# A planner that books small tiles and parameter tables in pieces of 2 or 4 columns instead of 128

## The chip, the cores and the metric

One core of one Trainium2 chip. The time is device microseconds (us) of one execution of the program. The engines: PE (TensorE, matmuls and transposes), DVE (VectorE), ACT (ScalarE), POOL (GpSimd), and SP (SyncE), whose queue issues the loads of the weights.

## The reference

A two-layer backbone in fp32 over 256 latent tokens of width 2048 and 256 context tokens. Layer 0 is neighbourhood attention beside a bidirectional state-space scan, with one common input projection; layer 1 is a gated short convolution. Both start with an adaptive norm.

```python
def adaln(cond, w, b):
    m = jax.nn.silu(cond) @ w + b
    return jnp.split(m, 3, axis=-1)

def reference(x, c, ctx, c_ctx, ada_w, ada_b, norm_g, ...):
    for i in range(DEPTH):                                  # DEPTH = 2
        ...
        shift, scale, gate = adaln(c, ada_w[i], ada_b[i])
        h = modulate(rms_norm(x, norm_g[i]), shift[:, None], scale[:, None])      # h*(1+scale)+shift
        if needs_ctx:                                       # layer 0
            shift_c, scale_c, gate_c = adaln(c_ctx, ada_w[i], ada_b[i])
            hc = modulate(rms_norm(ctx, norm_g[i]), shift_c, scale_c)
        if i % 2 == 0:
            y, yc = na_ssd_mixer(h, hc, na_ssd_w_in[e], ...)        # p = h @ w_in; pc = hc @ w_in[:, K..]
            # attention over a window and the context; softplus(dt + bias); scans both ways; @ w_out
        else:
            y = short_conv_mixer(h, sc_w_in[o], sc_conv_w[o], sc_w_out[o])
        x = x + gate[:, None] * y
    return x
```

## The kernel before

**Numbers.** Every fp32 weight block is split into a rounded high part `wH` (a cast on ACT, line L458) and a low part `wL` = weight - `wH` (a subtraction on DVE, L465). The activations have `hH` and `hL` likewise. A product is three matmuls into one PSUM bank: high by high, low by high, high by low. All matmuls are issued by the helper `mm` (L231), all transposes on PE by `turn` (L235), so that these two lines stand for nearly all of PE's work. In the rows of the trace the moving operand is named first, so `bank<-wH,hH` is a projection with the weights moving (K, V, Q) and `bank<-hH,wH` one with the tokens moving (B).

**Buffers.** Weights are loaded in blocks of 128 x 1024 (512 KB) into `raw` buffers (five, and at the start four more that lie in tiles used later: two `PT`, `xtm`, `yi`). Three pairs `wH`/`wL` hold the blocks in use. There are eight PSUM banks. `issue()` (L428) puts the next load into SP's queue as soon as the planner has given back a raw buffer.

**The order.** Nothing reorders the program after it is written: each engine's queue runs in the order in which the code emits instructions, and semaphores only make an engine wait. The emission order comes from a planner. The work is a fixed chain of matmul loops plus many small generators (tasks) in three queues (`urgent`, `side`, `back`); a task yields what it needs next, for instance `("DVE", tile)`, and `pump()` lets it go on once `may()` finds that the engine's booked time and the time at which the tile is ready lie near PE's booked time. `force()` runs the task that is ready first until a condition holds. Each emitted instruction is booked by `plan.add` (called `E`) with a cost; the class `Plan` keeps, per piece of a tile, the time at which it is written (`w`) and until when it is read (`r`). What a piece is, `Plan.keys` says: it turns the columns that an instruction touches into numbers of pieces of 128 columns. The planner's times decide the order and nothing else; the waits that keep the results right come from the tile framework.

**Tables.** `small` (436 columns, conditioning vectors, norm gains, biases) and `const` (866 columns: the identity, `mhalf` = 32 columns of -0.5 at columns 130 to 161, masks) come in two loads each: the first 96 columns of `small` and the first 162 of `const` at the very start, the rest (L565, L566) behind the tokens of the context. `rstd` (L604) computes 1/sqrt through `mhalf` on POOL.

**The first stage** (to about 110 us). `x_load`, `x_norm` and `x_pair` load four row tiles of tokens (t = 0, 1 latent, 2, 3 context), sum squares (L636 on ACT, L638 on DVE), scale them (`xs`, L648 and L650), transpose them (`turn`) and copy the result to `xm` (L663 ACT, L664 DVE). `ada_gen` goes through the modulation in blocks j = 0..7 of 256 columns, in two parts A (scale) and S (shift): 16 matmuls of 256 columns with `cpad` as weights, of which the trace shows each as two rows (in the order four raw buffers of a part, a row each), a copy to `half` (L768 ACT), two transposes of `half`, a reduction on DVE (L776) and adds (L779 to L782) into the 32-column tiles `A0` and `S0`; then for the two rows of block j `hH` = S + A x on ACT (L798), the same unrounded to `tmp` on DVE (L800), and `hL` = `tmp` - `hH` (L804). The main loop goes through the same j: K and V for four row tiles, Q for two, B; the partial results of K and V are added up in SBUF by `part_gen` (L828 copy for j = 0, L830 add on DVE from j = 1; K lies in `sz` and `gt`, V in `Vt`). `spawn(back, gemv_gen())` computes the later modulation rows on DVE (L857) with loads of its own.

**dt_gen** (about 230 to 260 us) turns the dt projection into softplus(dt + bias): it loads the 128-column table `rows` (L1184) into a `half` buffer, adds the projection's halves (L1201) and the table (L1203) and goes on with Abs, Exp and a series on DVE (L1209 to L1222; L1210 is a reciprocal).

Of the kernel before, what the change touches and what calls it, by code (L numbers as in the profile page):

```python
# [37 lines left out]
class Plan:  # L38
# [11 lines left out]
    def keys(self, ap):  # L50
        a, n = ap.ap, ap.tensor.name
        if type(ap.tensor).__name__ == "Tile" and not n.startswith("dram"):
            lo = ap.offset % a[0][0] if a[0][0] else ap.offset
            hi = lo + sum(abs(s) * (c - 1) for s, c in a[1:])
            return [(n, u) for u in range(lo // 128, hi // 128 + 1)]
        if n.startswith("in_") or n.startswith("out_"):
            return []
        hi = ap.offset + sum(abs(s) * (c - 1) for s, c in a)
        return [(n, u) for u in range(ap.offset // 256, hi // 256 + 1)]
# [1944 lines left out]
```

## Time and profile before

| what | value |
|---|---|
| three timed runs | 1763.7, 1769.15, 1769.4 us, median 1769.15 |
| the profiled execution | 1762.67 us |
| its span (first to last instruction) | 1760.9 us |
| busy share of the span: PE, DVE, ACT, POOL | 98%, 73%, 45%, 11% |
| moved by DMA | 412.5 MB, mean 234 GB/s |
| granted clock of TensorE, mean | 0.999 |

A profile row of a timeline has the start, the duration, the engine (SPq is SP's DMA queue, PEld the weight load of a matmul), the line, the operation, the outputs and inputs with shapes and types, the count, and in brackets the idle time ahead of it with what ended it. A row of the windows has the window, its length, the busy time and count of PE, PEld, DVE, ACT and POOL, the granted clock, the DMA share and GB/s. A row of the waits has the total, how many, and the longest. Matmuls overlap: one with 512 columns takes 0.39 to 0.5 in a row, but starts 0.23 after the one before it.

### The profile page before, as it was taken

The numbers are of one execution on the slowest core, as the hardware profiler recorded it, in microseconds if no ns is written. First come the engines' busy times: TensorE is split into PE (matmuls) and PEld (weight loads), VectorE is DVE, ScalarE is ACT, GpSimd is POOL, SyncE is SP. The second block draws the span as 40 slices with busy tenths as digits, with TensorE's granted clock in tenths as the row PEclk, the third lists the DMA queues.
The fourth block names the chain that finished last, engine by engine and source line by source line (L and its number), as shares of the span: only waits on it lengthen the run. The fifth ranks groups of instructions, "written<-read, shape, count | busy, mean of one in ns | idle before, by whom it ended". The sixth has DMA issues, their size and how long they took to land.

```text
span 1760.9 us, 25272 instructions
## 1 busy us (share of the span) xinstructions
PE 1728.3 (98%) x9305; PEld 1442.4 (82%) x9305; DVE 1292.8 (73%) x2041; ACT 785.3 (45%) x1186; POOL 191.0 (11%) x300
## 2 busy tenths in 40 slices
PE   6999999999999999999999999999999999999998
PEld 4677988889888889888888898888878888888887
DVE  5566877888787987786888698876667776766555
ACT  5422335454354453353453444654435444444442
POOL 0000111013111012111012101110000000000000
PEclk9999999999999999999999999999999999999999
DMA  9987675577876677866577767787766888876774
GB/s 349 344 291 252 214 227 181 181 214 241 261 227 201 190 219 248 262 193 204 170 239 227 215 188 226 224 261 253 268 216 232 265 281 266 267 248 216 219 231 158
DMA packets 147629, 412.50 MB, mean 234 GB/s; under 512 B 34304, under 2 KB 48272, under 8 KB 147504
## 3 DMA queue, kind: packets, MB, share of 16 engines
q1 hardware_dynamic: 132112, 366.64, 64.0%
q0 software_dynamic: 15392, 44.24, 8.0%
q8 instruction: 73, 1.20, 0.3%
q14 instruction: 52, 0.43, 0.1%
HBM read 386.53 MB, written 25.59 MB: 234 GB/s over the span
## 4 chain that ended last, share of the span: by engine, by line
PE 94%; DVE 2%; DMA 1%; ACT 1%; issue 1%; SPq 0%; POOL 0%; DVEq 0%; ACTq 0%; POOLq 0%
PE bank L231 93%; PE bank L235 1%; DVE wL L465 1%; DMA raw<-in_ada_w 0%; ACT wH L458 0%; DMA half<-in_rows 0%; DVE hL L804 0%; SPq L618 0%; DMA raw<-in_sc_in 0%; DVE tmp L1283 0%; DVE h L1729 0%; DVE tmp L800 0%; ACT h L1748 0%; ACT hH L798 0%; DVE xm L664 0%
## 5 line engine op out<-in xcount | busy, mean ns | idle before, releaser
L458 ACT CAST wH<-raw 128x1024 fp32r<-128x1024 f32 (+1 forms) x440 | 459.5, 1045 | 664.0 <-PE bank L231 559.6
L465 DVE TENSOR_TENSOR wL<-raw,wH 128x1024 fp32r<-128x1024 f32 (+1 forms) x440 | 532.2, 1213 | 257.4 <-ACT wH L458 255.0
L231 PE MATMUL bank<-hH,wH 128*128 128x256 f32 (+1 forms) x1040 | 341.0, 328 | 0.9 <-ACT wH L458 0.9
L231 PE MATMUL bank<-hL,wH 128*128 128x256 f32 (+1 forms) x1040 | 337.0, 324 | 0.0
L231 PE MATMUL bank<-hH,wL 128*128 128x256 f32 (+1 forms) x1024 | 331.4, 324 | 3.1 <-DVE wL L465 3.1
L231 PE MATMUL bank<-wH,h 128*128 128x512 f32 x1024 | 316.8, 390 | 1.7 <-DVE h L1729 1.7
L231 PE MATMUL bank<-wH,hH 128*128 128x512 f32 x640 | 256.0, 400 | 4.8 <-ACT hH L798 2.6
L231 PE MATMUL bank<-wL,hH 128*128 128x512 f32 x640 | 249.9, 391 | 0.3 <-DVE wL L465 0.3
L231 PE MATMUL bank<-wH,hL 128*128 128x512 f32 x640 | 249.3, 390 | 0.1
L231 PEld LDWEIGHTS bank<-wH,h 128*128 128x128 f32 x1024 | 191.9, 188 | 43.5 <-DVE h L1729 3.0
L231 PEld LDWEIGHTS bank<-hH,wH 128*128 128x128 f32 x1040 | 197.8, 190 | 18.9 <-issue 2.0
L231 PEld LDWEIGHTS bank<-hL,wH 128*128 128x128 f32 x1040 | 197.8, 190 | 15.8
L231 PEld LDWEIGHTS bank<-hH,wL 128*128 128x128 f32 x1024 | 194.6, 190 | 19.4 <-DVE wL L465 4.1
L857 DVE SCALAR_TENSOR_TENSOR acc<-raw,csil,acc 128x512 f32<-128x512 f32 x240 | 179.1, 746 | 30.9 <-DMA raw<-in_ada_w 27.2
L231 PE MATMUL bank<-wL,h 128*128 128x512 f32 x512 | 199.4, 389 | 0.2 <-DVE wL L465 0.2
L231 PE MATMUL bank<-wH,mix 128*128 128x512 f32 x512 | 160.9, 391 | 0.0
L231 PEld LDWEIGHTS bank<-wH,hH 128*128 128x128 f32 x640 | 120.1, 188 | 36.3 <-issue 7.2
L231 PEld LDWEIGHTS bank<-wH,hL 128*128 128x128 f32 x640 | 120.1, 188 | 25.4 <-DVE hL L804 0.6
L231 PEld LDWEIGHTS bank<-wL,hH 128*128 128x128 f32 x640 | 120.1, 188 | 25.0 <-DVE wL L465 1.1
L231 PEld LDWEIGHTS bank<-wL,h 128*128 128x128 f32 x512 | 96.1, 188 | 20.6 <-DVE wL L465 0.6
L231 PEld LDWEIGHTS bank<-wH,mix 128*128 128x128 f32 x512 | 96.1, 188 | 20.4 <-issue 0.5
L231 PE MATMUL bank<-wL,mix 128*128 128x512 f32 x256 | 99.7, 390 | 0.0
(276 smaller groups left out, 1856.5 us busy)
## 6 DMA issues: line engine op xcount, KB each, us to landing
raw<-in_w_in SPq DMA_DIRECT2D x209, 512.0 KB
raw<-in_ada_w SPq DMA_DIRECT2D x163, 512.0 KB
raw<-in_sc_in SPq DMA_DIRECT2D x128, 512.0 KB
raw<-in_w_out SPq DMA_DIRECT2D x64, 512.0 KB
raw<-in_sc_out SPq DMA_DIRECT2D x32, 512.0 KB
dram_ptd<-tmp POOLq DMA_DIRECT2D x32, 256.0 KB, 4.9
D<-dram_ptd POOLq DMA_DIRECT2D x64, 128.0 KB, 5.6
tmp<-dram_csr SPq DMA_DIRECT2D x32, 256.0 KB
```

Source lines behind the costliest of these rows:

```text
L231: E(T.matmul(o, l, r, start=start, stop=stop, skip_group_check=True))
L235: E(T.transpose(o, i, ident if k == 128 else ident[:k, :k]))
L458: E(S.copy(H, v))
L465: E(V.tensor_tensor(out=Lo, in0=v, in1=H.bitcast(F32), op=ALU.subtract))
L857: E(V.scalar_tensor_tensor(out=acc, in0=v[:, j], scalar=csil[:, 2 * k + j:2 * k + j + 1], in1=acc, op0=ALU.mult, op1=ALU.add))
```

## The change

`Plan.keys` cuts a tile into pieces of 4 columns if its rows are shorter than 256 elements (the sums of squares, `rx`, `A0`, `S0`, the statistics, the small rows of the gates), and of 2 columns if it is one of the two tables; all other tiles keep pieces of 128. The pieces of DRAM tiles, the kernel's arithmetic and the instructions are unchanged: each engine has the same ones as before.

```diff
         if type(ap.tensor).__name__ == "Tile" and not n.startswith("dram"):
             lo = ap.offset % a[0][0] if a[0][0] else ap.offset
             hi = lo + sum(abs(s) * (c - 1) for s, c in a[1:])
-            return [(n, u) for u in range(lo // 128, hi // 128 + 1)]
+            k = 4 if a[0][0] < 256 else 2 if n.startswith(("small", "const")) else 128
+            return [(n, u) for u in range(lo // k, hi // k + 1)]
```

With it a read of `mhalf` no longer counts as a read of the columns of `const` that the second load brings (from column 162, in the same 128 as 130 to 161), a read of `small`'s first columns no longer as one of those from 96 on, and the columns of `A0` and `S0` of block j are apart from those of the blocks ahead. The new file has one line more, so its line numbers are one higher from L56 on. Where the order differs, buffers also get other numbers.

PE, end of block 0 and start of block 1 of the first stage, before (`half_122` belongs to the A part of block 2, the last row is the first matmul of K for block 1):

```order
L231 MATMUL bank_134<-PT_153,cpad 32x256 x4
L231 MATMUL bank_134<-PT_154,cpad 32x256 x4
L231 MATMUL bank_134<-xtm,cpad 32x256 x4
L231 MATMUL bank_134<-yi,cpad 32x256 x4
L231 MATMUL bank_132<-hH_373,wH_140 128x512
L231 MATMUL bank_132<-hL_377,wH_140 128x512
L231 MATMUL bank_132<-hH_373,wL_143 128x512
L235 MATMUL bank_134<-const,half_122 128x128 x2
L231 MATMUL bank_129<-hH_373,wH_140 128x512
L231 MATMUL bank_129<-hL_377,wH_140 128x512
L231 MATMUL bank_129<-hH_373,wL_143 128x512
L231 MATMUL bank_127<-wH_141,hH_563 128x512
```

The same place after:

```order
L232 MATMUL bank_134<-xtm,cpad 32x256 x4
L232 MATMUL bank_134<-yi,cpad 32x256 x4
L232 MATMUL bank_134<-raw_135,cpad 32x256 x4
L232 MATMUL bank_134<-raw_136,cpad 32x256 x4
L232 MATMUL bank_133<-hH_373,wH_140 128x512
L232 MATMUL bank_133<-hL_377,wH_140 128x512
L232 MATMUL bank_133<-hH_373,wL_143 128x512
L236 MATMUL bank_134<-const,half_121 128x128 x2
L232 MATMUL bank_128<-wH_141,hH_608 128x512
L232 MATMUL bank_128<-wH_141,hL_613 128x512
L232 MATMUL bank_128<-wL_144,hH_608 128x512
L232 MATMUL bank_128<-wH_141,hH_615 128x512
```

Before, the transposes of `half_121` (part S of block 1) stand 38 rows further up, and the A part of block 2 comes ahead of K. After, part S of block 1 stands here: its matmuls (`xtm` to `raw_136`), its transposes, and directly behind them K of block 1. The transposes of all tokens (`const,xs`), which stood between the parts of block 1 before, now stand ahead of both.

ACT, from the copy of that part's matmuls to `hH` of block 1, before:

```order
L768 COPY half_121<-bank_132 128x256
L663 COPY xm_202<-bank_129 128x256
L663 COPY xm_204<-bank_133 128x256
L798 ACTIVATE hH_563<-xm_198,S_214,A_213 128x256 x2
L798 ACTIVATE hH_570<-xm_199,S_214,A_213 128x256 x2
```

The same place after:

```order
L769 COPY half_121<-bank_134 128x256
L459 CAST wH_141<-raw_138 128x1024
L459 CAST wH_142<-raw_139 128x1024
L799 ACTIVATE hH_608<-xm_198,S_214,A_213 128x256 x2
L799 ACTIVATE hH_615<-xm_199,S_214,A_213 128x256 x2
```

The casts of the weights of K and V of block 1 (`wH_141`, `wH_142`) now stand between the copy and `hH`; before, they came later, and two copies of tokens stood there. A little earlier on ACT, around the scaling of the fourth row tile (`xs_265`, `xs_269`), before:

```order
L636 ACTIVATE tmp_116,ssq<-xs_269 128x512
L828 COPY gt<-bank_129 128x512
L648 ACTIVATE xs_265<-xs_265,rx 128x512
L648 ACTIVATE xs_269<-xs_269,rx 128x512
L828 COPY Vt<-bank_132 128x512
L663 COPY xm_196<-bank_133 128x128
```

and after:

```order
L637 ACTIVATE tmp_116,ssq<-xs_269 128x512
L829 COPY gt<-bank_129 128x512
L829 COPY Vt<-bank_132 128x512
L649 ACTIVATE xs_265<-xs_265,rx 128x512
L649 ACTIVATE xs_269<-xs_269,rx 128x512
L664 COPY xm_196<-bank_133 128x128
```

The copy to `Vt` (from V's matmuls of the third row tile) has moved ahead of both scalings.

SP around the load of `rows` for the softplus, before:

```order
L1080 DMA bias_218<-dram_rpbs 64x4x64 x4
L428 DMA raw_139<-in_w_in 128x1024
L428 DMA raw_135<-in_w_in 128x1024
L428 DMA raw_136<-in_ada_w 128x1024
L428 DMA raw_138<-in_ada_w 128x1024
L428 DMA raw_137<-in_w_in 128x1024
L1184 DMA half_125<-in_rows 128x128
L428 DMA raw_139<-in_w_in 128x1024
```

and after:

```order
L1081 DMA bias_218<-dram_rpbs 64x4x64 x4
L429 DMA raw_139<-in_w_in 128x1024
L429 DMA raw_135<-in_w_in 128x1024
L429 DMA raw_136<-in_ada_w 128x1024
L1185 DMA half_125<-in_rows 128x128
L429 DMA raw_138<-in_w_in 128x1024
L429 DMA raw_137<-in_ada_w 128x1024
L429 DMA raw_139<-in_w_in 128x1024
```

Two of the five weight loads ahead of `in_rows` have moved behind it. Behind the add that needs this load DVE has, before, two low parts `wL_143` and `wL_144`, a transpose and `wL_145` ahead of the softplus:

```order
L1203 TENSOR_TENSOR half_126<-half_126,half_125 128x256
L465 TENSOR_TENSOR wL_143<-raw_139,wH_140 128x1024
L465 TENSOR_TENSOR wL_144<-raw_135,wH_141 128x1024
L250 STREAM_TRANSPOSE KT<-kqD_K_1984 128x4x4x32
L465 TENSOR_TENSOR wL_145<-raw_137,wH_142 128x1024
L250 STREAM_TRANSPOSE KT<-kqD_K_1984 128x4x4x32
L1209 TENSOR_SCALAR tmp_112<-tmp_112 128x256
L1210 RECIPROCAL tmp_112<-tmp_112 128x256
```

After, the first steps of the softplus stand between `wL_144` and `wL_145`:

```order
L1204 TENSOR_TENSOR half_126<-half_126,half_125 128x256
L466 TENSOR_TENSOR wL_143<-raw_139,wH_140 128x1024
L1086 TENSOR_TENSOR bias_218<-bias_218,const 128x512
L466 TENSOR_TENSOR wL_144<-raw_135,wH_141 128x1024
L1210 TENSOR_SCALAR tmp_110<-tmp_110 128x256
L1211 RECIPROCAL tmp_110<-tmp_110 128x256
L1213 TENSOR_TENSOR tmp_110<-tmp_110 128x256
L1214 TENSOR_TENSOR half_118<-tmp_110 128x256
L1215 TENSOR_SCALAR tmp_110<-half_118 128x256
L1218 SCALAR_TENSOR_TENSOR tmp_110<-tmp_110,half_118 128x256 x2
L466 TENSOR_TENSOR wL_145<-raw_138,wH_142 128x1024
L1218 SCALAR_TENSOR_TENSOR tmp_110<-tmp_110,half_118 128x256
```

## The prediction, written before the changed kernel ran

> **What bounds the kernel now.** I read the page first, then the table of windows, then PE's waits, then the timeline of the places that the waits name.
>
> ```profile
> span 1760.9 us, 25272 instructions
> ...
> PE 1728.3 (98%) x9305; PEld 1442.4 (82%) x9305; DVE 1292.8 (73%) x2041; ACT 785.3 (45%) x1186; POOL 191.0 (11%) x300
> ...
> L458 ACT CAST wH<-raw 128x1024 fp32r<-128x1024 f32 (+1 forms) x440 | 459.5, 1045 | 664.0 <-PE bank L231 559.6
> L465 DVE TENSOR_TENSOR wL<-raw,wH 128x1024 fp32r<-128x1024 f32 (+1 forms) x440 | 532.2, 1213 | 257.4 <-ACT wH L458 255.0
> ```
> ```profile
> 17.70:60.00 42.30, 37.28 (x292) 25.79 (x291) 26.87 (x71) 25.66 (x58) 1.61 (x4) 1.00 0.99 377
> 60.00:100.00 40.00, 37.74 (x261) 27.03 (x260) 23.76 (x44) 12.12 (x20) 0.00 (x0) 1.00 0.84 311
> 200.00:1300.00 1100.00, 1096.54 (x6099) 939.05 (x6099) 862.65 (x1419) 508.75 (x812) 156.55 (x235) 1.00 0.71 224
> 1756.00:1761.00 5.00, 0.00 (x0) 0.00 (x0) 1.38 (x3) 0.00 (x0) 0.00 (x0) 0.75 0.27 105
> ```
> ```profile
> PE bank L231 <- DVE rx L606: 13.1, 1, 13.1
> PE bank L231 <- DVE wL L465: 3.6, 5, 2.3
> PE bank L231 <- ACT hH L798: 2.6, 2, 1.4
> ...
> PE bank L231 <- DVE sz L830: 1.5, 1, 1.5
> ```
>
> TensorE is busy for 98% of the span at full clock; between 200 and 1300 us it is idle for 3.5 us of 1100 (1096.54 busy). The change adds no instruction to any queue: it only alters what the planner believes about small pieces, hence the order in which work stands. So a reordering can gain or lose only PE's waits. The largest, 13.1 us at the start (PE waits for the first norm), stands before the first row that moves. What is left to win is the short list under it; what there is to lose is a cover that is taken from a chain. Both sit between 36 and 100 us, where the DMA share is 0.99 and then 0.84, and at one place near 240 us. A step that runs 4 us late on ACT and DVE is free where PE has other rows ahead of the waiting one, and costs its full length where it has none. That is what I look for.
>
> **The change part by part. 1: block 1 of the first stage.** The planner used to see A0 and S0, 32 columns wide, as one piece each, and the tables' early columns as one with those that a second load brings. It now sees the four columns of a block apart and so finds work ready at other times. The order shows what it does with that: all x transposes (L235 with xs) come first, the ada(1) matmuls (cpad) slide behind them and behind two thirds of K0, V0 and B0, and the chain that makes hH and hL of block 1 starts right before the matmuls that need it.
>
> ```profile
> 39.54 1.34 ACT L648 ACTIVATE xs<-xs,rx 128x512 f32<-128x512 f32 x2 [0.26 <-POOL rx L607]
> 39.65 0.40 PE L231 MATMUL bank<-wL,hH 128*128 128x512 f32 x1
> 40.31 0.88 PE L235 MATMUL bank<-const,xs 128*128 128x128 f32 x6 [0.27 <-ACT xs L648]
> 40.78 0.56 ACT L828 COPY Vt<-bank 128x512 f32<-128x512 f32 x1
> 47.02 0.38 PE L235 MATMUL bank<-const,half 128*128 128x128 f32 x2
> 47.24 1.04 PE L235 MATMUL bank<-const,xs 128*128 128x128 f32 x8
> 47.98 2.08 ACT L798 ACTIVATE hH<-xm,S,A 128x256 fp32r<-128x256 f32 x4 [0.82 <-DVE S L782]
> 50.55 0.69 DVE L804 TENSOR_TENSOR hL<-tmp,hH 128x512 fp32r<-128x512 f32 x1
> 50.66 0.39 PE L231 MATMUL bank<-wL,hH 128*128 128x512 f32 x1
> 51.90 0.50 PE L231 MATMUL bank<-hH,wH 128*128 128x512 f32 x1 [0.85 <-ACT wH L458]
> 52.24 0.39 PE L231 MATMUL bank<-hL,wH 128*128 128x512 f32 x1
> 52.89 0.50 PE L231 MATMUL bank<-hH,wL 128*128 128x512 f32 x1 [0.25 <-DVE wL L465]
> 54.01 1.07 PE L231 MATMUL bank<-PT,cpad 128*32 128x256 f32 x16
> 55.87 0.50 PE L231 MATMUL bank<-hH,wH 128*128 128x512 f32 x1
> 57.59 0.39 PE L231 MATMUL bank<-wH,hH 128*128 128x512 f32 x1
> ```
>
> (PE's cpad matmuls for block 2's A part, 54.01 to 55.87, and two transposes, 2.1 us in sum, stand ahead of K1 before and behind its first nine matmuls now: work that only changes place.) Before, the last transposes of S (47.02) stand 10.6 us ahead of K1's first matmul (57.59), and the chain behind them (reduce, add, four hH on ACT, two hL on DVE) is done at 50.55 + 0.69 = 51.24, 4.22 us after they start: hidden. In the new order K1 follows these transposes at once. Two things lengthen the chain. ACT now has the casts of K1's and V1's weights between the copy to half and hH: 2 x 1.045 = 2.09 us, begun about 0.3 before the transposes (an estimate: the copy must end first), so hH starts at 1.8 instead of 47.98 - 47.02 = 0.96, 0.85 later. And DVE makes K1's wL behind both hL: 1.21. Chain: 4.22 + 0.85 + 1.21 = 6.3 us. PE has for cover the two transposes (47.02 to 47.24, 0.2) and K1's first two matmuls (0.23 each, as 57.59's kind run back to back): exposed 6.3 - 0.2 - 0.5 = 5.6. Its bounds: if the casts really come before the copy ends or hide in another wait, 4.7; if wL is late too by its cast, 6.5.
>
> **2: the rows just ahead of it.** On ACT the copy to Vt now stands ahead of both scalings of the fourth row tile (L648). It needs the matmul that starts at 39.65 and ends at 40.05, and takes 0.56, so the scaling starts at 40.65 instead of 39.54: PE's next transposes come 1.1 later, and nothing of PE's stands between. B0's low part (wL) stands behind the A half of ada(1) on DVE: I take 1.0 (from 0, if that half is early, to 2). One more wait for a bank, 0.3. What goes: the two waits in B0, 51.90 - 50.66 - 0.23 = 1.0 and 52.89 - 52.24 - 0.23 = 0.4. Together at K1: 5.6 + 1.1 + 1.0 + 0.3 - 1.4 = +6.6, with bounds +3.5 and +8.5.
>
> **3: banks in blocks 1 to 3.**
>
> ```profile
> 68.29 0.68 DVE L830 TENSOR_TENSOR gt<-gt,bank 128x512 f32<-128x512 f32 x1
> 69.03 0.50 PE L231 MATMUL bank<-wH,hH 128*128 128x512 f32 x1 [0.79 <-DVE gt L830]
> ...
> 87.19 1.22 DVE L465 TENSOR_TENSOR wL<-yi,wH 128x1024 fp32r<-128x1024 f32 x1
> 88.32 1.28 DVE L830 TENSOR_TENSOR sz<-sz,bank 128x512 f32<-128x512 f32 x2
> 89.06 0.50 PE L231 MATMUL bank<-wH,hH 128*128 128x512 f32 x1 [1.47 <-DVE sz L830]
> ```
>
> Twice PE waits for DVE to empty a bank (0.79 and 1.47) because a wL of 1.22 stands ahead of the evacuation. The new order shuffles wL, hL and evacuations here. Following it row by row with these durations I find the same kind of wait at two or three other places, 0.95, 1.55 and 0.85 in sum 3.35 against 2.26: +0.5 taken, since DVE, 23.76 busy of 40 us, can absorb half of the surplus; bounds -2.3 (all gone) and +2.
>
> **4: the row table before the softplus.**
>
> ```profile
> 232.44 1.02 SPq L428 DMA_DIRECT2D raw<-in_w_in  x2
> 233.55 0.86 SPq L428 DMA_DIRECT2D raw<-in_ada_w  x2
> 234.79 0.33 SPq L428 DMA_DIRECT2D raw<-in_w_in  x1
> 235.17 0.51 SPq L1184 DMA_DIRECT2D half<-in_rows  x1
> 242.40 0.43 DVE L1203 TENSOR_TENSOR half<-half,half 128x256 f32<-128x256 f32 x1 [6.09 <-DMA half<-in_rows]
> 242.74 2.35 DVE L465 TENSOR_TENSOR wL<-raw,wH 128x1024 fp32r<-128x1024 f32 x2
> 244.01 0.39 PE L231 MATMUL bank<-hH,wL 128*128 128x256 f32 x1 [2.33 <-DVE wL L465]
> 247.65 1.75 DVE L1210 RECIPROCAL tmp<-tmp 128x256 f32<-128x256 f32 x1
> ```
>
> DVE stands 6.09 us for the small table load (L1184), which SP issues behind five weight loads; the wL behind it on DVE is late, and PE waits 2.33. In the new order the load stands behind three, two 512 KB loads less in front of it. At the 377 GB/s of the window from 17.7 to 60 us one takes 1.4 us, so it lands about 2.8 earlier, near 239.5: DVE is free 2.8 earlier, more than PE's wait. Against that DVE now puts the first steps of the softplus (1.75 for the reciprocal, some 4 us in all) between two wL; I take 0.3 for it. -2.0, bounds -2.3 and +1.4 (the load as late as before, the softplus in front).
>
> **5: the rest.** Weight buffers of ada(1) come free up to 5 us later, so K1's and V1's loads are issued near 47 instead of 41.8. They are needed at about 55, behind the chain of part 1 in any case; I cost it at nothing as long as that chain is longer. If the chain is shorter, the loads are late next. Between 250 and 1750 us orders differ on DVE and ACT, but PE's total idle time there is a few us and nothing in the waits points at a moved row: 0, from -1 to +1.5. The end of the program (norm, last block, stores) is unmoved.
>
> **Sum:** +6.6 + 0.5 - 2.0 = +5.1 us. The profiled execution took 1762.67 (span 1760.9 and 1.8 around it); by it the changed kernel takes 1767.8. The three runs shown are 1763.7, 1769.15 and 1769.4, mean 1767.4, median 1769.15; the same kernel thus falls near 1763 or 1769. I put the sum on the mean: 1772.5. From no change a measurement here tells about 0.3%, 5.3 us, so my sum lies on that edge: a little slower, or the same.
>
> **The rivals.** *B, the chain costs more.* Either part 4's gain fails (sum 5.1 + 2.0), or the DMA hole is additive: with a share of 0.99 until 60 us the queue has no slack, and the 4 to 5 us in which no buffer is free push every later load back until PE meets them (+4). For it: the 0.99. Against it: 0.84 from 60 to 100, which gives back 6 us. A third way is the clock: in the 5 us after the last matmul the granted clock averages 0.75, so half of that time at half speed; an idle PE loses its clock, and if the pause at K1 does that too, some 2.5 us of the matmuls that follow run at half speed, +1.3 to +2.5. The 2.33 us wait near 244 left the clock at 1.00, and the pause of 5.6 is cut by K1's first two matmuls into pieces of about 2.1, 1.0 and 2.5. B gives +8 to +10: 1775.5 to 1777.5. [...]
>
> *C, the cover holds (not slower).* Its one mechanism: the A half's chain and the two casts run while PE is held up by part 2 anyway, and the transposes of S are issued early enough that K1's wL is ready when PE comes. It decides where wL of K1 is done less than 1.5 us after PE is through with the transposes; then part 1 costs 1.5 and not 5.6. Then 5.1 - 4.1 = +1, from -2 to +2: 1768.5. Against it: PE's own order puts the transposes of S and K1 side by side, and no engine can start the chain before them.
>
> *D, faster.* C with both bank waits (2.26) and the load's wait (2.33) gone and nothing in their place: 0 at part 1, -1.4 at part 2 (only what goes), -2.3 and -2.3 = -6.0: 1761.4. It decides where ACT and DVE run so far ahead that wL of K1 is done before PE asks for it; against it stands the same order of PE.
>
> *E, nothing:* the change may leave the order as it was. The order rows say it does not; this has no chance of its own.
>
> **How the numbers follow.** A, my forecast, +2 to +8: 0.55, half of it over 5.3. B 0.20, C 0.16, D 0.09. Slower: 0.28 + 0.20 = 0.48; faster: 0.09; same: the rest, 0.43. Range: from 1764 (C at the faster of the two levels) to 1781 (B on the slower one); D and the extremes of B are left out, some 2 in 10. A's own range is 1768 to 1777.
>
> **What would show it.** Right: PE's waits list an hL or wL of about 2 us at K1 near 58 to 62 us, twice, and hH there; ACT has two casts right before hH of block 1; K1's first matmul, then without block 2's A part ahead of it, near 58.6 (57.59 - 2.1 + 1.0 + 2.1), and its third, the first with wL, near 62; the wait for wL near 244 is gone and DVE's wait for in_rows is 4 us or less. Wrong: K1 within 2 us of 57.59; DMA waits on PE's weights between 60 and 100 us; a granted clock under 1.00 near 60 us; a wL wait of over 1 us near 245; or a new wait after 250 us that no row above names.

## The result and the profile after

The changed kernel takes 1785.8 us (median of 6 runs, 1782.9 to 1790.4) against 1768.5 before (6 runs, 1763.7 to 1770.9): ratio 1.0103, 95% interval 1.0084 to 1.0122. It is slower by 17 to 18 us, more than the range on record allowed. The profiled execution took 1786.8 with a span of 1785.0; the one of before (1762.67) lies at the fast end of its runs, so the two profiles differ by 24.1 us, 6 to 7 more than the medians.

The page and the windows of the changed kernel (line numbers are one higher than before):

```profile
PE 1739.6 (97%) x9305; PEld 1447.6 (81%) x9305; DVE 1293.4 (72%) x2041; ACT 787.1 (44%) x1186; POOL 191.1 (11%) x300
```
```profile
17.70:60.00 42.30, 34.15 (x250) 23.44 (x248) 22.95 (x65) 26.09 (x57) 1.60 (x4) 0.99 0.85 331
60.00:100.00 40.00, 37.49 (x248) 26.13 (x248) 22.36 (x42) 10.58 (x18) 0.00 (x0) 0.92 0.82 289
...
1000.00:1200.00 200.00, 195.16 (x1091) 167.16 (x1090) 150.09 (x264) 98.52 (x171) 23.51 (x36) 0.98 0.67 213
```

DVE and ACT do the same work as before. PE is "busy" for 11 us longer with the same 9305 instructions, which points to a lower clock: PEclk (third number from the right), 1.00 in all these windows before, is 0.99, 0.92 and 0.98 now. The third window in the profile before:

```profile
1000.00:1200.00 200.00, 199.39 (x1131) 171.54 (x1131) 159.94 (x270) 103.40 (x174) 22.49 (x35) 1.00 0.71 224
```

The waits of PE and DVE in the changed kernel:

```profile
PE bank L232 <- DVE wL L466: 7.4, 8, 2.3
PE bank L232 <- DVE tmp L1468: 5.7, 4, 2.3
PE bank L232 <- ACT hH L799: 3.9, 3, 1.8
...
PE bank L232 <- DVE gt L831: 1.4, 1, 1.4
```
```profile
DVE acc L858 <- DMA raw<-in_ada_w: 46.0, 28, 3.8
```

The second row is new: PE waits for the decay products of the scan (L1468; L1467 before), and DVE stands 28 times for loads of the later modulation rows, 46.0 us in sum. In the profile before that row read:

```profile
DVE acc L857 <- DMA raw<-in_ada_w: 27.2, 14, 3.8
```

Where the 24.1 us come from, by the start of the matmul that has k others ahead of it, in the two profiles: +0.3 for k = 0 (13.1 us before), +10.6 for 600 (101.6), +8.7 for 1200 (202.9), +6.0 for 1800 (302.4), +9.7 for 2400 (408.8), +10.2 for 4800 (836), +14.9 for 5700 (1002), +22.0 for 6300 (1091), +24.1 for 8100 (1485), and nothing after that. (Where the order differs a single value can be off by 2: around k = 600 they go from 8.0 to 10.6.) So the first stage costs about 8.3 (8.7 less the 0.3 of the start), the step at the row table's load gives 2.65 back near 244 us, and the rest, 18.1 in these two profiles, comes in steps between 300 and 1500 us, where I had put zero.

**The first stage** runs as drawn up. PE from the fourth row tile's transposes to the start of block 1:

```profile
41.20 3.49 PE L236 MATMUL bank<-const,xs 128*128 128x128 f32 x30 [1.30 <-ACT xs L649]
...
51.09 0.50 PE L232 MATMUL bank<-hH,wL 128*128 128x512 f32 x1 [0.70 <-DVE wL L466]
...
55.56 0.38 PE L236 MATMUL bank<-const,half 128*128 128x128 f32 x2
57.71 0.49 PE L232 MATMUL bank<-wH,hH 128*128 128x512 f32 x1 [1.77 <-ACT hH L799]
58.93 0.50 PE L232 MATMUL bank<-wH,hL 128*128 128x512 f32 x1 [0.72 <-DVE hL L805]
61.51 0.79 PE L232 MATMUL bank<-wL,hH 128*128 128x512 f32 x1 [2.08 <-DVE wL L466]
62.10 0.63 PE L232 MATMUL bank<-wH,hH 128*128 128x512 f32 x1
62.53 0.63 PE L232 MATMUL bank<-wH,hL 128*128 128x512 f32 x1
```

The two transposes of S, then hH (1.77), hL (0.72), wL (2.08), in this order and nearly in the sizes worked out. But behind them the matmuls start 0.43 us apart instead of 0.23, and last 0.63 instead of 0.39 to 0.40: the granted clock is 0.50 from 59.41 to 66.23.

**A typical step of the middle**, from the timeline near 400 us (DVE and PE):

```profile
399.96 1.54 DVE L858 SCALAR_TENSOR_TENSOR acc<-raw,csil,acc 128x512 f32<-128x512 f32 x2 [3.21 <-DMA raw<-in_ada_w]
...
401.42 0.61 DVE L1465 SCALAR_TENSOR_TENSOR tmp<-tmp,dtl,tmp 128x128 f32<-128x128 f32 x2
402.06 0.43 DVE L1468 TENSOR_TENSOR tmp<-tmp 128x256 f32<-128x256 f32 x1
...
402.54 0.65 PE L232 MATMUL bank<-tmp,xtm 128*64 128x128 f32 x6 [1.84 <-DVE tmp L1468]
```

DVE stands 3.21 us for a load of `ada_w` that only the background task `gemv_gen` needs; the scan's steps queue behind it; PE waits 1.84 for them. And there too the clock falls, to 0.50 (404.2 to 407.6 us). The same place before:

```profile
391.36 1.54 DVE L857 SCALAR_TENSOR_TENSOR acc<-raw,csil,acc 128x512 f32<-128x512 f32 x2 [0.53 <-DMA raw<-in_ada_w]
392.82 0.61 DVE L1464 SCALAR_TENSOR_TENSOR tmp<-tmp,dtl,tmp 128x128 f32<-128x128 f32 x2
393.46 0.42 DVE L1467 TENSOR_TENSOR tmp<-tmp 128x256 f32<-128x256 f32 x1
394.34 0.66 PE L231 MATMUL bank<-tmp,xtm 128*64 128x128 f32 x8
```

DVE's rows here stand in the same order in both kernels, the accumulation ahead of the scan's step. What differs is when the load has landed: DVE waits 0.53 us for it before, and PE does not wait. So a step that PE needs stood behind such a load before, too.

### The profile page after: what moved, and what is told of

It is laid out like the page before. It is cut to its first block, busy times and chain, and to the rows that moved or that the text cites. A ratio compares the mean times of both kernels' runs of the same rounds, so it can differ in the third digit from the quotient of the medians.

```text
span 1785.0 us, 25269 instructions
## 1 busy us (share of the span) xinstructions
PE 1739.6 (97%) x9305; PEld 1447.6 (81%) x9305; DVE 1293.4 (72%) x2041; ACT 787.1 (44%) x1186; POOL 191.1 (11%) x300
## 4 chain that ended last, share of the span: by engine, by line
PE 80%; DVE 5%; DMA 5%; issue 3%; ACT 1%; POOL 0%; DVEq 0%; POOLq 0%; ACTq 0%; SPq 0%
PE bank L232 79%; DMA raw<-in_ada_w 4%; DVE wL L466 2%; DVE acc L858 1%; PE bank L236 1%; DMA raw<-in_w_out 1%; ACT wH L459 1%; DVE tmp L1284 0%; DMA tmp<-dram_mrow 0%; DMA dram_kqd<-tmp 0%; DMA raw<-in_sc_in 0%; DVE D L1146 0%; DVE tmp L1465 0%; DVE h L1730 0%; POOL kqD_Q L246 0%
## 5 line engine op out<-in xcount | busy, mean ns | idle before, releaser
L858 DVE SCALAR_TENSOR_TENSOR acc<-raw,csil,acc 128x512 f32<-128x512 f32 x240 | 179.4, 748 | 49.7 <-DMA raw<-in_ada_w 46.0
```

Source lines behind the costliest of these rows:

```text
L858: E(V.scalar_tensor_tensor(out=acc, in0=v[:, j], scalar=csil[:, 2 * k + j:2 * k + j + 1], in1=acc, op0=ALU.mult, op1=ALU.add))
```

## The clock: what a wait costs beside itself

The profile's clock records show half speed in the changed kernel from 59.4 to 66.2, 404.2 to 407.6, 1042.4 to 1045.9 and 1107.3 to 1110.7 us; before, only after the last matmul. Three of these stretches last 3.413 us and one twice that, and they begin 101.0, 187.0 and 19.0 times 3.413 us apart; so in this profile they lie on one grid of cells of 3.413 us. Windows on that grid (behind the length comes PE's busy time; the clock is the third number from the right):

```profile
55.99:59.41 3.42, 0.97 (x2) 0.37 (x2) 2.30 (x7) 3.14 (x6) 0.00 (x0) 1.00 0.90 313
59.41:62.82 3.41, 1.33 (x4) 1.12 (x4) 3.08 (x4) 0.00 (x0) 0.00 (x0) 0.50 0.64 252
62.82:66.23 3.41, 3.41 (x21) 1.78 (x24) 0.69 (x1) 0.00 (x0) 0.00 (x0) 0.50 0.77 279
66.23:69.64 3.41, 3.41 (x35) 2.30 (x28) 0.94 (x4) 0.37 (x1) 0.00 (x0) 1.00 0.67 205
1103.89:1107.30 3.41, 1.10 (x10) 0.60 (x8) 2.23 (x6) 1.02 (x1) 0.00 (x0) 1.00 0.34 137
1107.30:1110.71 3.41, 3.41 (x10) 2.64 (x9) 3.37 (x8) 1.42 (x4) 0.71 (x1) 0.50 0.41 108
```

A cell in which PE worked 0.97 of 3.41 us (28%) is followed by a cell at 0.50; that cell again has little (1.33, 39%), and the next one, though full, is still slow; behind the full cell the clock is back at 1.00. The other three falls of this profile stand behind cells of 47%, 34% and 32% (from 400.74, 1039.03 and 1103.89 us); the least busy cell at full speed without a fall behind it has 59%. In the profile before the least busy cell has 57%, and the clock stays at 1.00 until after the last matmul. Counted in all 14 profiles of this case, each on its own grid, some 7170 cells from the first clock record to the last matmul: of the cells at full speed, each with PE busy for less than 50% is followed by half speed (22 of 22, from 11% to 49.7%), of six between 50% and 55% three are, and of all above just one, with 62%. Back to full speed it went after a cell of 98% or more (26 of 26), and after none of the six slow cells with 39% to 77%. The wait of 1.84 us near 400 us, which had a fall behind it, lies but for 0.04 in one cell, from 400.74 to 404.15. A longer one that two cells shared had none: the variant of the load on POOL's queue below has a wait of 2.32 us that ends at 305.59, split by the grid:

```profile
300.80:304.21 3.41, 2.47 (x21) 2.27 (x19) 3.31 (x5) 1.94 (x3) 0.00 (x0) 1.00 0.50 155
304.21:307.62 3.41, 2.03 (x17) 2.03 (x18) 3.41 (x5) 2.54 (x4) 0.00 (x0) 1.00 0.22 68
```

72% and 60% busy, and the clock stays at 1.00. Where the grid lies differs from profile to profile (the first clock record begins at 18.45 us in the changed kernel, at 17.70 before), and the falls near 404 and 1107 us are missing when the changed kernel ran again (run 5); I read this as the same pause costing a stretch of half clock in one run and none in the next, as it happens to lie on the grid. The runs of the kernel before fit that: of the 35 beside the last four experiments, the five with a mean clock of 1.000 took 1764 to 1767 us, the ten with 0.997 or less 1766 to 1776. That the grid makes this difference was not tested by itself.

## The experiments

The variants are built from the kernel before unless said otherwise; every ratio is against runs of the kernel before.

**The halves of the change, 1: only small tiles**

```diff
-            return [(n, u) for u in range(lo // 128, hi // 128 + 1)]
+            return [(n, u) for k in [4 if a[0][0] < 256 else 128] for u in range(lo // k, hi // k + 1)]
```

> Only the small tiles are booked in pieces of 4 columns, the two tables stay at 128. In the order the first stage is then as before, and from the load of the row table on it is as in the changed kernel. Theory (the loss has two separate parts, one per half of the change): 2.6 us gained near 244 us, about 14 us lost between 290 and 1350 us to DVE's waits for the loads of the modulation rows (acc) and to the clock, in sum +7 to +13 us, ratio 1.004 to 1.007, granted clock 1.00 at 60 us. Rival (all of it follows from the late start of block 1, which shifts every later load against the work): without that the middle is as before, and only the gain near 244 us is left: -2 to -3 us, ratio 0.998 to 0.999.

Measured: ratio 1.0046 (1.0030 to 1.0063), median 1777.6. Within the theory's range: first stage as before, 2.65 us gained near 244, and then

```profile
DVE acc L857 <- DMA raw<-in_ada_w: 48.1, 28, 5.2
```

as many waits as in the changed kernel, and clock falls at 1031 and 1117 us. A late start of block 1 is not needed for that.

**2: only the tables**

```diff
+            ... for k in [2 if n.startswith(("small", "const")) else 128] ...
```

> Only the two tables are booked in pieces of 2 columns, the small tiles stay at 128. The first stage then has the order of the changed kernel, the rest that of before. Theory: block 1's chain is exposed (waits of about 2, 1 and 2.3 us at K1) and the clock falls for two stretches of 3.4 us near 60: +8 to +10 us at 130 us, then the loss stays constant: ratio 1.004 to 1.006, and the wait near 244 us is still there. Rival (the middle is lost because of the late start): the ratio is that of the whole change, 1.009 to 1.011.

Measured: 1.0055 (1.0038 to 1.0072), median 1778.7. The theory's range again, and 1.0046 and 1.0055 together make 1.0101, beside 1.0103 for the whole; each interval is some 3 us wide to either side, so this does not exclude a share that belongs to both. The first stage is that of the changed kernel (waits of 1.93, 0.99 and 2.35 us beyond the normal distance of starts, clock 0.91 between 60 and 100 us). My expectation that the loss then stays constant failed in this profile: 8.3 us at k = 450 became 16.8 by k = 2700. Two low parts came late on DVE, and the clock fell behind both (at 254.9 and 319.7). The first is the one behind the row table: PE's wait there is 2.87 us, against 2.33 before. At the second, DVE stood 6.36 us for a modulation load, with its steps in the order of before:

```profile
310.25 1.54 DVE L857 SCALAR_TENSOR_TENSOR acc<-raw,csil,acc 128x512 f32<-128x512 f32 x2 [6.36 <-DMA raw<-in_ada_w]
...
319.33 0.39 PE L231 MATMUL bank<-hH,wL 128*128 128x256 f32 x1 [3.22 <-DVE wL L465]
```

The same step in the profile before:

```profile
295.67 1.54 DVE L857 SCALAR_TENSOR_TENSOR acc<-raw,csil,acc 128x512 f32<-128x512 f32 x2 [2.91 <-DMA raw<-in_ada_w]
```

So the rival has a part in it: a late start shifts loads against work even in the same order. How much of the 1.0055 that is in the mean of the runs, one profile does not tell.

**3 and 4: single small tiles.** Only `stat` (`... 4 if a[0][0] < 256 and n.startswith("stat") else 128 ...`):

> Of the small tiles only statk and statq (the sums of squares of the heads' K and Q) are booked in pieces of 4 columns. By the order this moves the loads and DVE steps of the modulation rows in 182 of 256 cases, and the other small tiles but s4 in none. Theory: if these moves carry the loss of the middle, +4 to +12 us, ratio 1.002 to 1.007. Rival (a move of so few pieces cannot matter, the softmax sums s4 do it): within 0.2% of before.

Measured: 1.0069 (1.0054 to 1.0083), median 1780.2: these two tiles alone cost at least about as much as all small tiles together (the intervals overlap). Only `s4_`:

> Of the small tiles only the softmax sums s4 are booked in pieces of 4 columns; by the order 99 of 256 modulation-row steps move. Theory: it is the reshuffle that costs and not one tile, so this one too loses a few us in the middle: ratio 1.001 to 1.005. Rival (only statk and statq matter): within 0.1% of before.

Measured: 1.0003 (0.9992 to 1.0014): no loss and no clock fall; the rival's number. DVE has 18 waits for the modulation loads here (37.1 us against 27.2 before), so their sum alone does not tell the cost. The pieces of `A0` and `S0`, which the prediction named as a reason, move nothing by themselves: with all small tiles in pieces of 4 (run 1) the first stage keeps the order of before, and with the tables alone (run 2) it has that of the changed kernel.

**5 and 6: the clock at K1.** The changed kernel again as the base:

> The changed kernel again (written on one line less, so that its lines carry the numbers of before), as the base for the two variants run beside it. Ratio 1.009 to 1.012 by every theory. If the clock falls at the end of stretches of a fixed grid in which PE was busy for less than about half, this profile shows falls only behind such stretches.

Measured: 1.0093 (1.0076 to 1.0109), median 1785.3. Its falls stand behind cells that were 29%, 36% and 50% busy (the last at 26.7 us, ahead of the first row of PE that moved), and the next lowest of the cells at full speed was at 57%. In this execution the clock does not fall near 404 and 1107 us. With matmuls put into the pauses (`fill(n)` issues n matmuls of 512 columns into a free bank):

```diff
+            f = (lambda n: fill(n)) if (j, key, t, k) == (1, "K", 0, 0) else (lambda n: None)
+            f(8)
             mm(ps, hH[kb][:, tt], HLo[0][:, k], first and k == 0, False)
+            f(3)
             mm(ps, hL[kb][:, tt], HLo[0][:, k], False, False)
+            f(9)
             mm(ps, hH[kb][:, tt], HLo[1][:, k], False, last and k == 1)
```

> The changed kernel with 20 idle matmuls (512 columns, into a free bank, results unused) put into PE's three waits at K1 of block 1: 8, 3 and 9, some 4.5 us of work into 5.3 us of waits. Theory (the pause makes the clock fall, and this costs 3.4 us beside the pause itself): clock 1.00 from 55 to 70 us, K1's matmuls 0.23 us apart, 3 to 4 us less than the changed kernel. Rival (the granted clock does not follow PE's work there, or the slow matmuls only eat up slack): as long as the changed kernel or up to 1 us longer.

Measured: 1.0080 (1.0060 to 1.0100), median 1783.2, 2.2 less than the base, where the theory had 3 to 4; the intervals are too wide to decide. The profiles decide: from 50 us to the end of the pauses the matmuls (the added ones left out) start within 0.04 us of each other in both; the waiting one with wL at 61.73 and 61.77; and then

```profile
61.77 0.50 PE L231 MATMUL bank<-wL,hH 128*128 128x512 f32 x1
62.11 0.40 PE L231 MATMUL bank<-wH,hH 128*128 128x512 f32 x1
62.35 0.40 PE L231 MATMUL bank<-wH,hL 128*128 128x512 f32 x1
```

full speed, 2.66 us ahead of the base at 70 us and still 2.4 at 694 us (later other waits differ). Twenty useless matmuls save 2.66 us; that is the clock's share of the first stage here.

**7 and 8 (control): DVE's waits for the modulation loads**

```diff
-  E(V.scalar_tensor_tensor(out=acc, in0=v[:, j], ...))
+  E(V.scalar_tensor_tensor(out=acc, in0=strip[:, :512], ...), <booked as before>)
```

> The changed kernel in the same order, but DVE's accumulation of the later modulation rows (L855, L857) reads a constant tile instead of the loaded weights, which are still loaded; so it leaves these modulation rows out of the computation and takes away DVE's waits for their loads (46 us in the profile). Theory (from 290 us on the loss comes from DVE standing behind these loads with the work of the scan and the low parts queued behind it): PE's waits for tmp at L1467 and most clock falls beyond 300 us go, 6 to 12 us less than the changed kernel. Rival (the steps of the scan are late by the new order in any case, DVE's wait for a load only fills idle time): within 2 us of it.

Measured: 1.0039 (1.0025 to 1.0054), median 1775.8, 9.5 us under the base of the same chip (5.7 between the two profiles, later other waits included). The wait of L1467 on PE (3.6 us in the base's profile) is gone. Near 400 us, the place shown above:

```profile
399.43 0.43 DVE L1467 TENSOR_TENSOR tmp<-tmp 128x256 f32<-128x256 f32 x1
...
400.94 0.66 PE L231 MATMUL bank<-tmp,xtm 128*64 128x128 f32 x8
```

the product is ready 1.1 us ahead of PE. My expectation that most clock falls beyond 300 us would go did not come true: the base's profile has falls at 60.8 and 1040.4, and this one at 60.8 and 1037.0, the latter behind a low part queued after the convolution's steps. The edit takes away something else as well: a load into a raw buffer no longer waits until DVE has read it (104 waits of SP for L857, 129.0 us in the base). I see no gain from that: SP waits longer for the low parts instead (1012.4 us against 902.9), and ACT's casts wait for weights as long as before (25.6 us against 23.5). The same edit in the kernel before, which frees the buffers in the same way:

> The kernel before in its own order, with DVE's accumulation of the modulation rows reading a constant tile (these modulation rows are left out of the computation, their loads stay): the control to the same edit of the changed kernel, which gained 9.5 us. Theory (before, DVE's waits for these loads, 27 us, fall where PE has cover): 0 to 2 us less than before, ratio 0.999 to 1.000. Rival (the waits for the loads cost before as much, and the edit gains in any order): 6 to 10 us less, ratio 0.995.

Measured: 0.9990 (0.9978 to 1.0003): there these waits (27.2 us) cost nothing that can be told, and the freed buffers gain nothing. So it is not waiting for the loads as such that costs, but a wait that is long enough, at a place ahead of a step that PE needs, to make PE wait. What is left after the edit, 7.0 us over the kernel before, is mostly the first stage less the gain at 244 us (8.3 - 2.65 = 5.7); the remaining 1 to 2 us stay open.

**9 and 10: nudges that have nothing to do with pieces** (`RATE = 270.0` to 268.0 and 272.0):

> The kernel before with the pieces untouched and another nudge to the planner: its DMA rate is 268 instead of 270 (0.7%). By the order some 1260 of 1830 DVE rows change places, as many as with the small tiles. Theory (before stands in an order that happens to be good, and any nudge that reshuffles the middle loses there): ratio 1.003 to 1.008, more waits of DVE for the modulation rows' loads than the 14 of before. Rival (it is the finer pieces that mislead the planner): within 0.2% of before.

> The same with 272, which moves only some 150 DVE rows. Theory: a small reshuffle, a small loss: ratio 0.999 to 1.003. Rival: as before within 0.1%.

Measured: 1.0035 (1.0022 to 1.0047) and 1.0038 (1.0022 to 1.0054). The first is as the theory has it, with the same signature:

```profile
DVE acc L857 <- DMA raw<-in_ada_w: 52.6, 26, 6.5
```

The second, which moves few rows, was put at 0.999 to 1.003 and lost as much. Its profile shows no more waits for modulation loads than that of `s4_`, which loses nothing (18 waits, 29.6 us), but waits of PE of 2.5 us up to 244.8 and 1.8 up to 488.7, and clock falls at 245.7 and 771.4. So a loss of this size does not need finer pieces; of five nudges tried in the middle (small tiles, `stat`, `s4_`, two rates) four lose 0.35 to 0.7% and none gains.

**11 and 12: a better kernel**

```diff
-        E(DMA.dma_start(rw[:, :128], rows[0].partition_broadcast(128)))
+        E(G.dma_start(rw[:, :128], rows[0].partition_broadcast(128)))
```

> The kernel before with one edit: the load of the row table (L1184) goes through POOL's queue instead of SP's, and stands behind no weight load there; every other row is in its old place. Theory (DVE's wait of 6.1 us for this load and PE's wait of 2.3 us behind it go): 2.3 to 3.5 us less than before, ratio 0.998 to 0.9987. Rival (the wait moves to the next low part): within 0.5 us.

Measured: 0.9977 (0.9965 to 0.9989), median 1764.7: 4.1 us faster than before (forecast 2.3 to 3.5), the best of all kernels here, and the order of everything else is untouched. POOL and DVE at that place:

```profile
224.20 0.59 POOL L1184 DMA_DIRECT2D half<-in_rows  x1
...
237.06 0.42 DVE L1201 TENSOR_TENSOR half<-bank,half 128x256 f32<-128x256 f32 x1
237.52 0.43 DVE L1203 TENSOR_TENSOR half<-half,half 128x256 f32<-128x256 f32 x1
```

No wait between the two adds, where 6.09 us stood. The load itself is not faster: it lands 8.2 us after its issue here, and before DVE could go on 7.2 us after the issue (235.17 to 242.40). What changed is the issue: POOL comes to it at 224.20, SP at 235.17, because SP first has to issue the eight loads of the bias and the five of weights (from 225.08 on). This profile does not account for the whole 4.1 us: it gains 1.7 near 244 and loses 2.5 near 305, at the wait shown above; that the rest is a clock that no longer falls behind the row table in some runs is possible (it fell there in the profiles of runs 2 and 10, at 254.9 and 245.7) and not shown. With the modulation steps held back in the planner as well:

> A try at a better kernel: before with the row table's load on POOL's queue (which gained 4 us) and, in the planner, the modulation rows' steps held back until 2 us instead of 1 us after their load is booked to land. Theory: fewer waits of DVE for these loads (under 20 us instead of 33), ratio 0.994 to 0.998 if the new order brings nothing else. Rival (any reshuffle of the middle costs what it gains): 0.998 to 1.003.

Measured: 0.9986 (0.9975 to 0.9996). DVE's waits for the loads fell from 17 (32.6 us) to 11 (25.2 us), not under the 20 us expected, and the new order brought a wait of 3.6 us in the second norm and a clock fall at 1312 us: not better than the one edit alone.

## Why the prediction was wrong, step by step

- **The sign was right** (slower at 0.48), the size was not: +5.1 forecast, +17.3 measured by the medians. Term by term: first stage +7.1 forecast and +8.3 measured, row table -2.0 and -2.65 (both measured in the two profiles), everything behind it 0 and some +11.6 (what is left of the 17.3). Two of the signs that I had named for being wrong came: a clock under 1.00 near 60 us, and new waits after 250 us.
- **Part 1, the exposed chain, held.** Forecast 5.6 us of waiting at K1 in pieces of 2.1, 1.0 and 2.5; the rows have 1.77, 0.72 and 2.08, in starts 1.93, 0.99 and 2.35 (sum 5.3). The third matmul was put near 62 us, it starts at 61.51. K1's first matmul was put near 58.6 and starts at 57.71. That is within 2 us of 57.59, which I had named as a sign of being wrong; but so was my own 58.6, so that sign could not tell the two apart.
- **Part 2 held.** PE waits 1.30 for the fourth row tile's scaling instead of 0.27 (1.0 more, forecast 1.1); B0's low part is waited for by 0.70 (forecast 1.0).
- **Part 3 held within its bounds:** the two bank waits moved (1.4 for gt and 0.8 for sz, together as much as the 0.79 and 1.47 before), so its +0.5 did not come.
- **Part 4 held in its number:** DVE waits 2.88 us for the table instead of 6.09, PE's wait is gone, 2.65 us are gained (forecast 2.0, at most 2.3). The reason was half right. I had counted the transfers ahead of the load; but from its issue (241.76) to the add (248.03) it still takes 6.3 us instead of 7.2. The rest is that SP comes to it earlier, with two loads fewer to issue ahead of it (241.76 against 235.17, where the program stands 8.7 us later than before).
- **The clock was a term of rival B and belonged into the sum.** I set against it that two matmuls divide the pause into pieces, and that the 2.33 us near 244 had left the clock alone. In the rows the divided pause left two cells in a row at 28% and 39%, and the clock was 0.50 from 59.41 to 66.23; the 2.33 us were shared by two cells of 62% and 70%. Forecast for the case +1.3 to +2.5; the filler measured 2.66 at this place alone, and the profile has three further falls. That the first stage came out near its forecast (8.3 for 7.1) is in part luck: without the clock it is 5.6, so waits put 1.5 too high made up for more than half of the clock that was left out.
- **The step that failed is part 5:** "Between 250 and 1750 us orders differ on DVE and ACT, but ... nothing in the waits points at a moved row: 0, from -1 to +1.5". It cost some 11 us by the runs of the small tiles (1.0046 is 8.1 us, net of the 2.65 gained), and 13 to 18 in the four profiles that have all small tiles in fine pieces (the changed kernel, runs 1, 5 and 6), each against a profile of before that is itself some 6 us under its median. I had read that PE hardly waits there, and took it for slack. It showed only that in this order nothing was late. DVE's row of 14 waits for modulation loads, 27.2 us, was there to be read: each is a place where a step that PE needs can stand behind a load that is late; and most of DVE's rows moved. Taking these waits away gave 9.5 us back (run 7), so they are the larger part of the step; in the changed kernel's first profile two of the clock falls (404.2 and 1107.3) stand behind such waits. DVE's longest wait for such a load is between 3.8 and 6.5 us in the runs that lose by them, so the planner places these steps by up to that much too early; that any reshuffle deals such places anew is how I read the five nudges, four of which lose.
- **The two parts can be had one by one:** the tables make the first stage's loss, `statk` and `statq` alone make one in the middle; but the late start of the tables' half has some share in the middle, too (run 2). By the code, the planner before held each of K's four reductions back behind the one ahead, since all wrote to one piece; that this small shift is what starts the reshuffle is argued, not shown.

## What to carry to other kernels

When a change only moves instructions, a stage without waits is not a stage with slack: count on each engine's queue the waits that are hidden now (here DVE's for late loads), and ask for each moved row what would stand behind it. Price a pause of the matmul engine at itself plus the clock: behind K1's waits (5.3 us in sum) two slow cells cost a measured 2.66 us; behind the 1.84 us near 400 us one cell was slow, and such a cell full of work costs 1.7 by my estimate (half of the 3.413 us measured). A small load that an engine waits for should not stand behind many others in the queue of the engine that issues it: moving one table to another queue had it issued 11 us earlier and, with no other row moved, was worth 4 us, more than any reordering here.

## What the runs showed of the hardware that I had not expected

- In the 14 profiles the clock fell to 0.50 after 22 of 22 cells of a 3.413 us grid in which PE was busy for less than 50% (11% at the least, so none was idle), after 3 of 6 with 50% to 55%, and after one above (62%); it came back after 26 of 26 cells of 98% or more, and after none of six slow ones with 39% to 77%.
- At a granted clock of 0.50 a 512-column matmul started 0.43 us after the one before (62.10 to 62.53) instead of 0.23, and PE's busy time rose from 1728.3 to 1739.6 us with the same 9305 instructions: the "busier" PE is the slower one here.
- Doing 20 useless matmuls in K1's waits gave 2.66 us back (run 6).
- The 64 KB load of the row table took 8.2 us from its issue to its landing on POOL's queue (run 11), and on SP's 7.2 until DVE went on (before); the queue decided when it was issued (224.20 or 235.17 us), not how long it took.
